# Seven products instead of eight blocks for a third pair of w_down blocks, and the query tiles in a shared pool

## The chip, the cores and the metric

The kernel runs on one core of one Trainium2 chip, in one launch. The metric is the device time in microseconds (us). The engines named here are TensorE (PE in the rows, its weight loads PEld), VectorE (DVE), ScalarE (ACT), GpSimd (POOL), and SyncE (SP), which issues most of the DMAs.

## What is computed

Two layers of a trunk with three token mixers, an MLP and an embedding gate, all in fp32. The change lies in the MLP; its other half moves two tiles of the attention branch. The reference, cut to these:

```python
for i in range(DEPTH):                       # DEPTH = 2, h is (1, 256, 1024)
    u = rms_norm(h, norm_mix_g[i])
    proj = u @ w_in[i]
    ...                                      # pooling, gated convolution, differential attention (q, k, v)
    h = h + merged @ w_o[i]
    m = rms_norm(h, norm_mlp_g[i])
    h = h + jnp.square(jax.nn.relu(m @ w_up[i])) @ w_down[i]      # 1024 -> 4096 -> 1024
    e = rms_norm(h, norm_ple_g[i])
    h = h + jax.nn.sigmoid(e @ w_ple_gate[i]) * (p[i] @ w_ple_proj[i])
```

## The kernel before

Every product of fp32 numbers is made from three: an operand is split into a rounded high part and the remainder, and high by high, high by low and low by high are summed in PSUM. Activations are split once. Weights are streamed from HBM and split on the way: `WeightStream` loads them in transfers of two units of 128x1024 numbers into three staging buffers; for each unit ACT copies the high part (`whi`, L285) and DVE subtracts it (`wlo`, L286). The two parts go to one of six buffers (`AHEAD + 1`, L197, L207), so a unit is split up to five units ahead of its matmuls, and its buffer is free once the unit six places before it has been read. `weight_plan` lists the units in the order in which PE takes them; transfers are issued in that order.

The MLP of a layer has eight blocks b of 512 hidden columns. Block 0 comes first, in four units of their own shape. For each other block there are four "up" units, `("up", b, m)`, of 128 hidden columns: 16 matmuls (`unit_c`, L487) into one PSUM bank of the pool `bp`, which has four banks. `relu_sq_c` (L1128) follows an up unit: ACT copies the bank, and after the second of two units DVE adds, ACT does a relu and two squares, and DVE subtracts; this leaves the block's squared activations as a high part and a remainder (`st["s", b]`), and, for a block whose pair is in `GROUPS`, the squares themselves (`st["f", b]`).

The way back down has two forms. Directly, `("down", b, f)` is two units of kind A, each 12 matmuls of 512 columns (`unit_a`, L436), for one half f of the output columns; a block has two of these. A pair of blocks j, j+1 whose j is in `GROUPS` is done by Strassen's seven products `("S", j, n)` instead of eight block products: each product is two units of kind S, each six matmuls of 512 columns (`unit_s`, L459). Around the products stand

- four operands of the activations (`operands`, L1169, steps 0 to 3, for products 5, 6, 3 and 7 in that order): a sum or difference on DVE, a copy of its high part on ACT (L537), the remainder on DVE (L538). They are attached to the four units that follow the last up unit of block j+1;
- the weights. Products 2 and 3 use plain blocks through the staging buffers. The others use two 1 MB tiles, `self.sums`: two blocks are loaded into them (L233), DVE adds them after product 1 was split (L265), and POOL issues DMAs that add further blocks to them (`add_to`, L256), one after the split of each of the products 1, 5 and 6. The tiles are free for the next pair (`sums_busy`) once product 4 has been split; until then `load` (L219) stops at the next pair's product 1;
- what happens to the results (`product_out`, L1212): products 1, 6 and 7 run up one sum in one bank ("chain"), from which DVE takes parts after each; product 5 is copied by ACT; 2, 3 and 4 go into the accumulators of the direct units.

Before the change the pairs (0,1) and (4,5) are done so, the blocks 2, 3, 6 and 7 directly, and `mlp_order` (L59) writes the order of ups, products and downs out by hand. Side work is attached to a unit and comes in program order behind it; the Tile framework then orders the instructions of each engine by a priority that follows the program, and gives out buffers from pools. `u4` (8 buffers) holds tiles of 128x1088 numbers: the split and squared activations, the copies of the up units, and in the mixers the operands of the branches. The split queries `qT` are two constant tiles of their own, written in `qk_transpose` (L659) and read in `probs` (L736).

## Time and profile before

| what | value |
|---|---|
| time, median of 3 runs | 841.7 us (841.66 to 843.43) |
| time of the profiled execution | 842.62 us |
| its span | 840.7 us |
| PE busy | 832.3 us, 99% |
| DVE busy | 669.1 us, 80% |
| ACT busy | 563.9 us, 67% |
| TensorE clock granted | 1.00 in all forty slices |
| moved by DMA | 177.29 MB, 211 GB/s |

The span is the time from the first to the last instruction that the profiler saw; the profiled execution's own time is 1.9 us longer. The share of an engine is its busy time over the span. Matmuls are pipelined, so that the times of single matmuls overlap: what one costs is read from the distance of two starts.

### The profile page before, as it was taken

The numbers are of one execution on the slowest core, as the hardware profiler recorded it, in microseconds if no ns is written. First come the engines' busy times: TensorE is split into PE (matmuls) and PEld (weight loads), VectorE is DVE, ScalarE is ACT, GpSimd is POOL, SyncE is SP. The second block draws the span as 40 slices with busy tenths as digits, with TensorE's granted clock in tenths as the row PEclk, the third lists the DMA queues.
The fourth block names the chain that finished last, engine by engine and source line by source line (L and its number), as shares of the span: only waits on it lengthen the run. The fifth ranks groups of instructions, "written<-read, shape, count | busy, mean of one in ns | idle before, by whom it ended". The sixth has DMA issues, their size and how long they took to land.

```text
span 840.7 us, 11223 instructions
## 1 busy us (share of the span) xinstructions
PE 832.3 (99%) x4236; PEld 706.5 (84%) x4236; DVE 669.1 (80%) x926; ACT 563.9 (67%) x821; POOL 46.2 (5%) x52
## 2 busy tenths in 40 slices
PE   8999999999999999999999999999999999999997
PEld 7888888788988888888878888888889888888886
DVE  5989989876679667977678798998766886688864
ACT  6867566654678667976666756666546876688662
POOL 2400000000000000000023000000000000000000
PEclk9999999999999999999999999999999999999999
DMA  9864539764758766966546455586655778668531
GB/s 330 308 232 150 226 107 293 209 217 177 272 161 262 243 241 186 266 195 209 184 165 223 172 170 232 137 244 220 216 184 226 249 208 256 244 200 245 191 133 51
DMA packets 27126, 177.29 MB, mean 211 GB/s; under 512 B 3136, under 2 KB 4032, under 8 KB 6464
## 3 DMA queue, kind: packets, MB, share of 16 engines
q1 hardware_dynamic: 24192, 157.53, 51.3%
q0 software_dynamic: 2592, 18.88, 12.0%
q8 instruction: 33, 0.54, 0.2%
q10 hardware_dynamic: 288, 0.18, 0.1%
q14 instruction: 21, 0.17, 0.1%
HBM read 175.52 MB, written 1.05 MB: 210 GB/s over the span
## 4 chain that ended last, share of the span: by engine, by line
PE 97%; DMA 1%; ACT 1%; DVE 0%; issue 0%; ACTq 0%
PE acc L445 38%; PE bp L493 19%; PE bp L495 10%; PE bp L445 6%; PE acc L464 3%; PE acc L466 3%; PE acc L468 3%; PE acc L456 2%; PE bp L468 2%; PE bp L466 2%; PE bp L464 2%; PE tr L516 1%; PE acc L1309 1%; PE bp L482 1%; PE bp L484 1%; PE bp L480 1%
## 5 line engine op out<-in xcount | busy, mean ns | idle before, releaser
L286 DVE TENSOR_TENSOR wlo<-stage,whi 128x1024 fp32r<-128x1024 f32 (+1 forms) x272 | 328.3, 1213 | 111.2 <-ACT whi L285 109.7
L285 ACT CAST whi<-stage 128x1024 fp32r<-128x1024 f32 (+1 forms) x272 | 282.8, 1045 | 188.6 <-PE acc L445 81.7
L445 PE MATMUL acc<-whi,t 128*128 128x512 f32 x928 | 299.0, 392 | 0.0
L445 PEld LDWEIGHTS acc<-whi,t 128*128 128x128 f32 x928 | 173.6, 188 | 34.9 <-ACT whi L285 0.2
L493 PE MATMUL bp<-t,whi 128*128 128x512 f32 x704 | 192.3, 394 | 0.0
L445 PE MATMUL acc<-wlo,t 128*128 128x512 f32 x464 | 181.4, 391 | 0.0
L493 PEld LDWEIGHTS bp<-t,whi 128*128 128x128 f32 x704 | 122.2, 189 | 18.0
L495 PEld LDWEIGHTS bp<-t,wlo 128*128 128x128 f32 x704 | 107.9, 189 | 14.7
L495 PE MATMUL bp<-t,wlo 128*128 128x256 f32 x704 | 112.4, 281 | 0.0
L445 PEld LDWEIGHTS acc<-wlo,t 128*128 128x128 f32 x464 | 87.2, 188 | 17.3 <-DVE wlo L286 0.2
L286 DVE TENSOR_TENSOR wlo<-t,whi 128x1024 fp32r<-128x1024 f32 x60 | 73.0, 1221 | 14.7 <-ACT whi L285 13.7
L285 ACT CAST whi<-t 128x1024 fp32r<-128x1024 f32 x60 | 63.0, 1052 | 29.6 <-PE acc L445 9.3
L256 POOL DMA_DIRECT2D t<-in_w_dram x18 | 15.9, 884 | 474.5 <-DVE wlo L286 159.1
L464 PE MATMUL acc<-whi,t 128*128 128x512 f32 x104 | 40.6, 391 | 0.3 <-ACT t L989 0.3
L445 PE MATMUL bp<-whi,t 128*128 128x512 f32 x128 | 40.7, 389 | 0.0
L466 PE MATMUL acc<-wlo,t 128*128 128x512 f32 x104 | 40.6, 390 | 0.0
L468 PE MATMUL acc<-whi,t 128*128 128x512 f32 x104 | 40.5, 390 | 0.0
L506 ACT ACTIVATE t<-tr,par 128x256 fp32r<-128x256 f32 (+1 forms) x56 | 26.2, 501 | 15.0 <-PE tr L516 11.0
L507 DVE SCALAR_TENSOR_TENSOR t<-tr,par,t 128x256 fp32r<-128x256 f32 (+1 forms) x56 | 27.9, 525 | 6.8 <-ACT t L506 6.5
L1135 ACT COPY t<-bp 128x512 f32<-128x512 f32 x56 | 32.1, 577 | 0.0
L445 PEld LDWEIGHTS bp<-whi,t 128*128 128x128 f32 x128 | 24.0, 188 | 5.1 <-ACT t L537 0.2
L468 PE MATMUL bp<-whi,t 128*128 128x512 f32 x64 | 25.1, 393 | 0.0
(178 smaller groups left out, 1004.3 us busy)
## 6 DMA issues: line engine op xcount, KB each, us to landing
stage<-in_w_dram SPq DMA_DIRECT2D x131, 1024.0 KB, 4.8
t<-in_w_dram POOLq DMA_DIRECT2D x18, 1024.0 KB, 8.5
t<-in_w_dram SPq DMA_DIRECT2D x12, 1024.0 KB, 6.0
stage<-in_w_dram SPq DMA_DIRECT2D x6, 512.0 KB, 5.8
stage<-in_w_dram SPq DMA_DIRECT2D x4, 256.0 KB, 4.3
h<-in_x_dram SPq DMA_DIRECT2D x4, 256.0 KB, 10.2
t<-in_xT_dram SPq DMA_DIRECT2D x1, 512.0 KB, 8.6
out_dram<-h SPq DMA_DIRECT2D x2, 256.0 KB, 2.0
```

Source lines behind the costliest of these rows:

```text
L285: self.nc.scalar.copy(out=hi[:, cs], in_=src[:, cs])
L286: self.nc.vector.tensor_sub(out=lo[:, cs], in0=src[:, cs], in1=hi[:, cs].bitcast(F32))
L445: nc.tensor.matmul(accs[t], lhsT=lhs[:, kx + j, tk], rhs=rhs[:, j, :], start=begins[t] and j == 0 and n == 0, stop=last and j == 1 and n == 2,
L456: nc.tensor.matmul(accs[half][t], lhsT=lhs[:, k, t * P:(t + 1) * P], rhs=rhs[:, 0, cs], start=k == 0 and n == 0, stop=False)
L464: nc.tensor.matmul(bank, lhsT=xh[:, k + n, :], rhs=wh[:, n, :], start=first, stop=False, skip_group_check=True)
L466: nc.tensor.matmul(bank, lhsT=xh[:, k + n, :], rhs=wl[:, n, :], start=False, stop=False, skip_group_check=True)
L468: nc.tensor.matmul(bank, lhsT=xl[:, k + n, :], rhs=wh[:, n, :], start=False, stop=k + n == 3, skip_group_check=True)
L493: nc.tensor.matmul(bank, lhsT=wh[:, k, :], rhs=xk[k], start=k == 0, stop=False, skip_group_check=True)
L495: nc.tensor.matmul(bank[:, 1, :], lhsT=wl[:, k, :], rhs=xk[k][:, 0, :], start=False, stop=k == KD - 1, skip_group_check=True)
L506: nc.scalar.activation(out=hi, in_=src, func=AF.Copy, scale=g)
L507: nc.vector.scalar_tensor_tensor(out=lo, in0=src, scalar=g, in1=hi.bitcast(F32), op0=ALU.mult, op1=ALU.subtract)
L1135: nc.scalar.copy(out=both[:, :, m % 2, :], in_=tiles.pop(("bp", "up", j, m)))
```

## The change

- `GROUPS` gains the pair (2,3). Per layer eight A units of w_down (blocks 2 and 3, both halves, two units each) go, and seven products of two S units each come, with their operands, weight sums and results. The blocks 6 and 7 stay direct.
- `mlp_order` is written anew: `up(b, *ms)` names single up units, and the 21 products stand between them, mostly behind one or two up units each.
- `qT` is allocated from `u4` in each layer, when the first queries are written, and `u4` has ten buffers instead of eight.

```diff
--- before.py
+++ after.py
@@ -32,7 +32,7 @@
 UNIT_COLS = {"A": 512, "B": 256, "C": 128, "D": 1024, "P": 512, "S": 512}
 
 
-GROUPS = (0, 4)
+GROUPS = (0, 2, 4)
 
 GATED = 0
 
@@ -58,8 +58,8 @@
 
 def mlp_order():
 
-    def up(b, half):
-        return [("up", b, m) for m in (2 * half, 2 * half + 1)]
+    def up(b, *ms):
+        return [("up", b, m) for m in ms]
 
     def down(b, f):
         return [("down", b, f)]
@@ -67,13 +67,14 @@
     def prod(j, *ns):
         return [("S", j, n) for n in ns]
 
-    order = up(0, 0) + up(0, 1) + up(1, 0) + up(1, 1)
-    order += up(2, 0) + prod(0, 1) + up(2, 1) + up(3, 0) + prod(0, 5) + down(2, 0) + up(3, 1) + prod(0, 3)
-    order += down(2, 1) + prod(0, 6) + down(3, 0) + up(4, 0) + prod(0, 7) + down(3, 1) + prod(0, 2)
-    order += up(4, 1) + up(5, 0) + prod(0, 4) + up(5, 1)
-    order += up(6, 0) + prod(4, 1) + up(6, 1) + prod(4, 5) + up(7, 0) + prod(4, 3) + up(7, 1) + prod(4, 6)
-    order += down(6, 0) + prod(4, 7, 2) + down(6, 1) + prod(4, 4) + down(7, 0) + down(7, 1)
-    return order
+    order = up(0, 0, 1, 2, 3) + up(1, 0, 1) + prod(0, 1) + up(1, 2, 3) + up(2, 0, 1) + prod(0, 5) + up(2, 2) + prod(0, 3)
+    order += up(2, 3) + up(3, 0) + prod(0, 6) + up(3, 1) + prod(0, 7) + up(3, 2) + prod(0, 2) + up(3, 3) + prod(0, 4)
+    order += up(4, 0, 1) + prod(2, 1) + up(4, 2, 3) + prod(2, 5) + up(5, 0) + prod(2, 3) + up(5, 1, 2) + prod(2, 6)
+    order += up(5, 3) + prod(2, 7) + up(6, 0) + prod(2, 2) + up(6, 1, 2) + prod(2, 4)
+    order += up(6, 3) + prod(4, 1) + up(7, 0, 1) + prod(4, 5) + up(7, 2) + prod(4, 3) + up(7, 3) + down(6, 0)
+    order += prod(4, 6) + down(6, 1) + prod(4, 7, 2)
+    return order + prod(4, 4) + down(7, 0) + down(7, 1)
+
 
 
 A_IN, C_X, C_B, C_C, Q, K, V, GATE = (MIX * i for i in range(8))
@@ -339,7 +340,7 @@
     const = ctx.enter_context(tc.tile_pool(name="const", bufs=1))
     ws = WeightStream(ctx, tc, w)
     u8 = ctx.enter_context(tc.tile_pool(name="u8", bufs=4))
-    u4 = ctx.enter_context(tc.tile_pool(name="u4", bufs=8))
+    u4 = ctx.enter_context(tc.tile_pool(name="u4", bufs=10))
     u2 = ctx.enter_context(tc.tile_pool(name="u2", bufs=17))
     sm = ctx.enter_context(tc.tile_pool(name="sm", bufs=4))
     ps_acc = ctx.enter_context(tc.tile_pool(name="ps_acc", bufs=4, space=bass.MemoryType.PSUM))
@@ -412,7 +413,6 @@
     invcnt = csb[:, CC_INV:CC_INV + 4 * PAD].rearrange("p (g t) -> p g t", t=PAD)
     mhalf = const.tile([P, 16], F32, tag="mhalf", name="mhalf")
     nc.gpsimd.memset(mhalf, -0.5)
-    qT = [const.tile([P, NH, S], F32R, tag=f"qT{j}", name=f"qT{j}") for j in range(2)]
 
 
     lam = const.tile([P, DEPTH], F32, tag="lam", name="lam")
@@ -660,6 +660,9 @@
             tk = slice(t * P, (t + 1) * P)
             tr = head_transpose(qkr.pop((nm, t)))
             if nm == "q":
+                if t == 0:
+                    st["qT"] = [t4v(F32R) for _ in range(2)]
+                qT = st["qT"]
                 gain_split(qT[0][:, :, tk], qT[1][:, :, tk], tr, par[:, i, PC_QG:PC_QG + 1])
                 return
             for a in range(2):
@@ -738,7 +741,7 @@
             nk = (t + 1) * P
             scv = acc_tile().rearrange("p (h a k) -> p h a k", h=nh, a=2)
             for n, hd in enumerate(heads):
-                qh, ql = [q[:, hd, t * P:(t + 1) * P] for q in qT]
+                qh, ql = [q[:, hd, t * P:(t + 1) * P] for q in st["qT"]]
                 kh, kl = [k[:, hd, :, 0:nk] for k in st["kp"]]
                 nc.tensor.matmul(scv[:, n], lhsT=qh, rhs=kh, start=True, stop=False)
                 nc.tensor.matmul(scv[:, n], lhsT=qh, rhs=kl, start=False, stop=False)
```

## Rows read from the trace of the kernel before

**Rows 1.** the page: busy time of each engine, and the chain's shares by engine

```profile
PE 832.3 (99%) x4236; PEld 706.5 (84%) x4236; DVE 669.1 (80%) x926; ACT 563.9 (67%) x821; POOL 46.2 (5%) x52
...
PE 97%; DMA 1%; ACT 1%; DVE 0%; issue 0%; ACTq 0%
```

**Rows 2.** waits of PE, whole span: engine, line, awaited; us, times, longest

```profile
PE acc L456 <- ACT t L506: 1.7, 2, 1.2
...
PE acc L464 <- ACT t L989: 0.3, 1, 0.3
```

**Rows 3.** chain of work in order of time: start us, us, what

```profile
281.06 5.44 PE acc L445 x24
```

**Rows 4.** timeline of PE around one product: start us, us, engine line

```profile
308.30 0.39 PE L464 MATMUL acc<-whi,t 128*128 128x512 f32 x1
...
311.01 1.07 PE L493 MATMUL bp<-t,whi 128*128 128x512 f32 x4
```

**Rows 5.** timeline of all engines, from up(1,3)'s end to pair 0's first operand

```profile
244.74 1.09 PE L493 MATMUL bp<-t,whi 128*128 128x512 f32 x4
...
246.87 0.68 DVE L1141 TENSOR_TENSOR t<-t 128x512 f32<-128x512 f32 x1
...
247.55 1.09 PE L493 MATMUL bp<-t,whi 128*128 128x512 f32 x4
...
250.35 0.40 PE L464 MATMUL bp<-whi,t 128*128 128x512 f32 x1
...
250.56 0.70 DVE L1146 TENSOR_TENSOR t<-t,t 128x512 fp32r<-128x512 f32 x1 [0.97 <-ACT t L1145]
...
251.17 0.69 DVE L1175 TENSOR_TENSOR t<-t,t 128x512 f32<-128x512 f32 x1
...
252.91 0.61 ACT L537 CAST t<-t 128x512 fp32r<-128x512 f32 x1
...
253.12 1.07 PE L493 MATMUL bp<-t,whi 128*128 128x512 f32 x4
...
254.17 1.21 DVE L286 TENSOR_TENSOR wlo<-t,whi 128x1024 fp32r<-128x1024 f32 x1
...
255.30 0.68 DVE L538 TENSOR_TENSOR t<-t,t 128x512 fp32r<-128x512 f32 x1
```

**Rows 6.** DVE by form, MLP of layer 0 (222 to 386 us)

```profile
L286 DVE TENSOR_TENSOR wlo<-stage,whi 128x1024 fp32r<-128x1024 f32 x53 | 64.4, 1222 | 21.0 <-ACT whi L285 20.6
...
L265 DVE TENSOR_TENSOR t<-t,t 128x2048 f32<-128x2048 f32 x2 | 4.6, 2289 | 0.0
...
L1209 DVE SCALAR_TENSOR_TENSOR h<-bp,r,h 128x512 f32<-128x512 f32 x4 | 3.0, 743 | 0.0
```

**Rows 7.** busy time by stretch: PE, PEld, DVE, ACT, POOL, clock, DMA

```profile
222.00:386.00 164.00, 164.00 (x872) 141.15 (x871) 130.10 (x143) 121.20 (x166) 5.25 (x6) 1.00 0.71 224
...
340.00:360.00 20.00, 20.00 (x110) 17.20 (x109) 19.00 (x24) 18.51 (x28) 0.88 (x1) 1.00 0.91 242
```

**Rows 8.** timeline of PE in the first up units: order of issue

```profile
230.05 0.28 PE L480 MATMUL bp<-t,whi 128*128 128x256 f32 x1
230.17 1.09 PE L493 MATMUL bp<-t,whi 128*128 128x512 f32 x4
231.10 0.28 PE L482 MATMUL bp<-t,whi 128*128 128x256 f32 x1
```

**Rows 9.** the page: DMA queues; the commonest load, its median us to landing

```profile
q1 hardware_dynamic: 24192, 157.53, 51.3%
q0 software_dynamic: 2592, 18.88, 12.0%
...
stage<-in_w_dram SPq DMA_DIRECT2D x131, 1024.0 KB, 4.8
```

**Rows 10.** timeline of SP's queue: the two loads of pair 4's sums

```profile
291.97 0.33 SPq L233 DMA_DIRECT2D t<-in_w_dram  x1
...
313.56 0.33 SPq L233 DMA_DIRECT2D t<-in_w_dram  x1
```

## The prediction, made before the changed kernel was run

> **What bounds the kernel now.** I read the busy times first, then the waits of PE, then the chain, and only then single stretches. PE is busy for 99% of the span and makes 97% of the chain that ended last [rows 1]. Busy time alone would prove little, because the times of pipelined matmuls overlap; so the second view matters more: in the whole span PE waited five times, 3.8 us in all (the largest 1.7, the smallest 0.3), each time in a stage that the change does not touch [rows 2]. In both MLPs it never waits. There the spacing of matmuls is the time: 24 matmuls of 512 columns take 5.44 us, 0.227 us each [rows 3]. DVE is the next engine: 130 of 164 us in the MLP of layer 0, 79%, and 19 of 20 us in its fullest stretch, where PE still does not wait [rows 7]. So matmuls that vanish shorten the kernel one for one, as long as DVE, ACT and the DMAs still keep ahead. The whole question is whether they do.
>
> **What PE loses.** Eight A units go per layer. An A unit is 12 matmuls, half of the 5.44 us of 24: 2.72 us [rows 3]; eight are 21.8. Seven products come, 12 matmuls each. A product behind a direct unit takes 2.71 us [rows 4], one behind an up unit 2.77 (250.35 to 253.12) [rows 5]. In the new order nearly every product stands behind an up unit, so 7 x 2.77 = 19.4. The difference is 2.4 us per layer, 4.8 for two. The bounds: 2.7 per layer if the switch between shapes costs nothing more, 2.1 if all 21 products pay 0.06 more than they did and nothing is given back. I take 4.8.
>
> By the Trainium skill's page "TensorE: Matmul & The Clock Gate" (Back-to-back issue gap) a sustained stream of 512-column matmuls is spaced about 131 ns; 24 fewer would then give an estimate of 3.1 us instead of 5.4. The row disagrees: 227 ns here, with PE waiting for nothing.
>
> **What DVE gains in work, per layer.** From starts that follow one another without idling: a weight remainder 1.13 us (254.17 to 255.30), a 512-column operation 0.61 (250.56 to 251.17) [rows 5]; the big weight sum 2.29 and a residual update 0.74 by their durations [rows 6]. Six more units to split (14 for 8): 6.8. Four operands, two operations each: 4.9. Results of products 1, 6 and 7: four residual updates and two additions, 4.2. One weight sum: 2.3. Together 18.2, on 130: 148 of some 162 us, 91%.
>
> The mean hides where it falls. Take the stretch from the end of pair 0's product 1 to the end of pair 2's product 4, 47 units. PE needs 21 up units x 2.81 (244.74 to 247.55 [rows 5]) + 13 products x 2.77 = 95.0. DVE needs 47 remainders (53.1), ten relu pairs (12.2), twelve operands, since pair 4's fall in here too (14.6), seven residual updates and four additions of results (7.6), two weight sums (4.6): 92.1, or 97%. Against this stands the lead: a unit is split five units ahead. Five units of this stretch (two ups, three halves of products) last 9.7 us, less 2.3 for the copy and the remainder: about 7 us by which DVE may be late. Adding the same durations unit by unit in the new order, and taking off what PE needs for each, its backlog comes to at most 5 us, around pair 2's products 7 and 2. So I cost the work on DVE at nothing; its cover is that lead. ACT gets six copies of some 1 us and five shorter ones, 9 on 121 [rows 7]: 80%, likewise nothing.
>
> **What the DMAs gain.** On SP nothing in bytes: eight half-megabyte units go, two loads of sums and two staged megabytes come. On POOL three adding DMAs per layer, 3.1 MB. POOL's queue took 12.0% of 840.7 us for 18.9 MB [rows 9], 5.3 us per MB, so 17 us per layer; the share of the engines in the MLP rises from 0.71 to about 0.82. A stretch at 0.91 made no wait [rows 7]. Nothing.
>
> **What is moved closer.** Four distances shrink.
> 1. *Pair 0's first operand.* Before, from the end of up(1,3) at 244.74 to the end of the remainder at 255.98 it took 11.2 us: relu chain to 251.17, then sum, copy and remainder, 2.8 us of it queued behind other work on ACT and DVE [rows 5]. Product 5 came far later, so nobody waited. Now only up(2,0) and up(2,1) stand between: 5.6 us, plus 0.5 until the remainder is read, 6.1. The chain is short by 2.3 (nothing queued) to 5.2 us (as before). But PE's order is not the program's: four matmuls of up(1,0) were issued in the midst of block 0's last units [rows 8], because the framework fills a gap that it foresees with later work that is ready. up(2,2), 2.81 us, is ready behind product 5. With it the loss is 0 to 2.4 us per layer, to 5.2 without.
> 2. *Product 7 behind product 6* waits until DVE has taken the sum from the bank; one up unit, 2.81 us, stands between in pairs 0 and 2. A remainder that is under way and the addition are 1.13 + 0.61 = 1.7. Nothing, with 1.1 to spare; a loss as large as DVE's further lateness without it.
> 3. *The weight sums are reloaded* for pair 4 with one up unit between pair 2's product 4 and its product 1. Split of product 4, a load of 4.8 us [rows 9], the next split of 2.3: 7.1, against 7.4 + 1.4 + 2.8 = 11.6 with full lead. It spares 4.5, about DVE's backlog there; a loss of 0 to 2 us per layer. The second sum is free earlier and was loaded 21.6 us before the first [rows 10], so one megabyte counts, not two.
> 4. *Pool of ten.* At up(4,1) the split activations of blocks 2, 3 and 4, three tiles of squares and one copy are alive: ten, just enough. In the mixers ten less two queries are the eight of before. Nothing; the cover is that PE has no wait there.
>
> For 1 to 3 together I take 0.5 us per layer, near the lower ends, since PE's order bends and DVE was caught up in most places. Sum: 840.7 - 4.8 + 1.0 = 836.9 of span; with the 1.9 us around it 838.8 against 842.6 of this execution. That execution is 0.9 above the median, so 837.9 against 841.7.
>
> **The rivals.**
> - *The operand is late* (point 1). For it: 11.2 us against 6.1 and nothing in the edit that speeds the chain. Against it: rows 8, and two more buffers, so copies of up units may come sooner. With up(2,2) taken ahead at most 2.4 us per layer are lost, about what is won: 840 to 842.5. Without it 10.4 - 4.8: 847.
> - *DVE becomes the bound, and it is slower.* Place: the 47 units. DVE seldom runs without holes, since remainders wait for ACT's copies (21 us idle before 53 of them [rows 6]). If it can be filled only to 85%, between the 79% of the MLP and the 95% of the fullest 20 us, it needs 108.4 us; less 95.0 and the lead of 7, that is 6.4 lost per layer: 841.7 - 4.8 + 12.8 = 849.7. It decides at 88%: below that the loss exceeds 2.4. Against it: 95% for 20 us without a wait. The Trainium skill's "Perfetto Trace Analysis" (Identifying the Most-Contended Engine) judges TensorE by its weight loads, not by matmul time; by this PE has 16% of headroom (84% in rows 1), and DVE, at 91% of the MLP, would be the engine to relieve, not to load. The missing waits of PE speak against it.
> - *The reload of sums* (point 3), up to 2 us per layer: 838 to 841.
> - *It does not do what it says:* a pool that is one short or a wait in the mixers eats the gain: 841 to 843.
>
> **How the numbers follow.** Forecast, stalls of up to 1.7 us per layer: 836.3 to 839.9, chance 0.64. Late operand in part, reload or pool: 840 to 843, 0.21. Late operand in full 0.05, DVE as the bound 0.10: 845 to 850. About 0.2% (1.7 us) is what a measurement of this kernel can tell from no change. So faster 0.65, same 0.21, slower 0.14. The range leaves out the last two cases and goes down to 835.8, all of 2.7 per layer and no stall with some spread.
>
> **What would show it.** PE should have 24 matmuls fewer and 5 us less busy time; each MLP should be 1.5 to 2.4 us shorter. PE's waits should name little in the MLP: L538 or L537 before pair 0's product 5 is rival one; `wlo` spread over the blocks 3 to 6 is rival two; `whi` before pair 4's product 1, with a load behind it, is the reload. DVE should be at 90% or more of the MLP. I am wrong in the mechanism if the matmuls go and PE's waits in the MLP grow to more than 2.4 us per layer.

## The result, and the profile after

The changed kernel takes 854.68 us (median, 853.80 to 855.66) against 842.57 us (841.66 to 843.51) for the kernel before, taken beside it: a ratio of 1.0145, interval 1.0133 to 1.0158. It is slower by 12.1 us where a gain of 3.8 was forecast. The profiled execution took 854.15 us with a span of 852.3, 11.6 more than before. In the rows of the changed kernel a line of before has a number that is 1 higher up to L414, the same from there to L660, and 3 higher behind it.

The page, the rows that answer to [rows 1] and [rows 9]: busy time, DMA queues, and the commonest loads (their last number is the median time to landing).

```profile
PE 832.6 (98%) x4212; PEld 705.9 (83%) x4212; DVE 701.0 (82%) x968; ACT 574.9 (67%) x843; POOL 54.8 (6%) x58
...
q1 hardware_dynamic: 25632, 157.53, 49.9%
q0 software_dynamic: 3456, 25.17, 15.6%
...
stage<-in_w_dram SPq DMA_DIRECT2D x117, 1024.0 KB, 4.9
t<-in_w_dram POOLq DMA_DIRECT2D x24, 1024.0 KB, 8.8
```

The 24 matmuls are gone (4212 for 4236), the six adding DMAs have come. By the page alone little else is new: every engine's share moved by 2 points at most, and the medians to landing lie within 0.3 us of those of before (4.8 and 8.5). The waits of PE tell more (engine, line, awaited: us in total, times, longest), beside [rows 2]:

```profile
PE bp L464 <- ACT whi L286: 4.2, 1, 4.2
PE bp L464 <- ACT t L537: 3.8, 2, 1.9
PE bp L493 <- ACT t L1138: 2.6, 1, 2.6
PE acc L464 <- ACT t L992: 1.8, 2, 1.3
PE acc L464 <- ACT whi L286: 1.4, 1, 1.4
PE tr L394 <- POOL mhalf L415: 1.0, 1, 1.0
PE acc L456 <- ACT t L506: 0.5, 1, 0.5
```

They add up to 15.3 us against 3.8. The first three rows are in the MLP, where PE had not waited: before pair 0's product 5 in both layers (1.89 us each), and in pair 2 (2.63 us at 308 in layer 0, 4.17 us at 734 in layer 1). The next two rows are three waits at the gates of the mixers (1.26 us in layer 0, 1.45 and 0.50 in layer 1). Then the stretches around the two waits in pair 2, in the columns of [rows 7] (the number after POOL's count is the granted clock, then the DMA share), with the whole MLP of layer 0 first:

```profile
222.00:386.00 164.00, 159.48 (x842) 136.91 (x841) 141.12 (x160) 125.05 (x175) 7.86 (x9) 0.99 0.76 231
300.00:320.00 20.00, 17.37 (x85) 14.56 (x84) 16.58 (x22) 13.46 (x21) 1.54 (x2) 0.91 0.93 252
720.00:740.00 20.00, 15.83 (x72) 13.17 (x71) 15.94 (x19) 11.81 (x18) 1.73 (x2) 0.83 0.90 247
```

In them the clock was granted at 0.91 and 0.83, where all slices of before had 1.00. That is the lower of the two levels, 1.2 GHz, for some microseconds; it began shortly behind the end of the wait in layer 0 and shortly before it in layer 1. The loss is 20 x 0.09 and 20 x 0.17 us, 5.1 together before rounding. In layer 1 the lower level began 1.2 us before the wait ended, and half of that is no loss of its own, so that some 4.5 us come on top of the waits (1.7 and 2.8). On PE's timeline of layer 0 one sees both, the wait and then a group of four matmuls that takes 1.91 us where the same group took 1.09 in [rows 5]:

```profile
308.01 1.19 PE L493 MATMUL bp<-t,whi 128*128 128x512 f32 x4 [2.63 <-ACT t L1138]
309.04 0.75 PE L495 MATMUL bp<-t,wlo 128*128 128x256 f32 x4
309.59 1.91 PE L493 MATMUL bp<-t,whi 128*128 128x512 f32 x4
```

So the 11.6 us of span come out: 11.5 more of waits, 4.5 of half clock, and by subtraction 4.4 less for the rest, which is near the 4.8 forecast for the matmuls.

Why PE waited at 308.01 stands on ACT's timeline:

```profile
301.87 0.62 ACT L1148 ACTIVATE t<-t 128x512 f32<-128x512 f32 x1
306.43 1.04 ACT L286 CAST whi<-stage 128x1024 fp32r<-128x1024 f32 x1 [3.95 <-DMA stage<-in_w_dram]
307.38 0.58 ACT L1138 COPY t<-bp 128x512 f32<-128x512 f32 x1
...
312.47 2.00 ACT L286 CAST whi<-t 128x1024 fp32r<-128x1024 f32 x2 [2.56 <-DMA t<-in_w_dram]
```

ACT kept to its order. From 302.5 it stood still before the copy of a weight unit that PE would need only at 312.15, because its load had not landed; the copy that empties a PSUM bank (L1138) stood behind it, and PE had no free bank. Of ACT's waits in the MLP of layer 0, 18.1 us are for DMAs:

```profile
ACT whi L286 <- DMA stage<-in_w_dram: 10.6, 5, 3.9
ACT whi L286 <- DMA t<-in_w_dram: 7.5, 4, 3.0
```

In the MLP of layer 0 before there was no such wait, in layer 1 one of 2.8 us, at which PE did not wait. And 7.0 of the 18.1 us come after 340 us, in pair 4, where PE does not wait either; so such a wait cost time here only where what stood behind it in ACT's order was what PE needed next. In layer 1 PE's wait is of the other kind: ACT waited 3.34 us until 732.75 for the addition that makes product 6's sum (issued at 720.26, landed after 12.42 us), and PE for ACT. The load that was late in layer 0 was issued at 296.05, between pair 2's first two adding DMAs, here POOL's timeline from 290 to 325:

```profile
295.42 0.87 POOL L257 DMA_DIRECT2D t<-in_w_dram  x1 [29.26 <-DVE t L266]
299.79 0.88 POOL L257 DMA_DIRECT2D t<-in_w_dram  x1 [3.50 <-DVE wlo L287]
316.21 0.87 POOL L257 DMA_DIRECT2D t<-in_w_dram  x1 [15.54 <-DVE wlo L287]
```

In the kernel before, POOL's timeline from 320 to 350 shows the first two additions of pair 4:

```profile
330.36 0.88 POOL L256 DMA_DIRECT2D t<-in_w_dram  x1 [49.01 <-DVE t L265]
339.11 0.88 POOL L256 DMA_DIRECT2D t<-in_w_dram  x1 [7.88 <-DVE wlo L286]
```

There they are 8.75 us apart, and the first landed after 8.62 us, before the second was issued. Now the two are 4.4 us apart, so the second is issued while the first is under way. By the trace they landed after 10.73 and 12.61 us, and the load between them after 10.30, where the median of such a load is 4.9. The view of the DMAs from 290 to 306 us, cut to it, shows the same: a line of 40 slices of 0.4 us with the busy share in tenths, and the issues in that stretch.

```profile
DMA  0000000010000000099359919879593996949299
...
t<-in_w_dram POOLq DMA_DIRECT2D x2, 1024.0 KB, 11.7
stage<-in_w_dram SPq DMA_DIRECT2D x1, 1024.0 KB, 10.3
```

For the first 6.8 us almost nothing moves, since the staging buffers were full: from 280 to 310 us SP's queue waited for DVE to be done with one, once for 9.8 us.

```profile
SPq L251 <- DVE wlo L287: 22.7, 4, 9.8
```

Then two additions and the loads come at once. A share averaged over 20 us shows neither the hole nor the heap.

The changed kernel's own pair 4 shows that the heap alone is not enough. POOL's timeline there:

```profile
347.36 0.88 POOL L257 DMA_DIRECT2D t<-in_w_dram  x1 [30.28 <-DVE t L266]
353.60 0.87 POOL L257 DMA_DIRECT2D t<-in_w_dram  x1 [5.36 <-DVE wlo L287]
```

The stretch behind it, in the columns of [rows 7]:

```profile
360.00:380.00 20.00, 20.00 (x93) 16.62 (x92) 15.64 (x18) 15.12 (x21) 0.87 (x1) 1.00 1.01 317
```

These additions overlap too (6.2 us apart, 8.72 and 10.74 us to landing), the loads issued beside them took 8.02 to 10.06 us, the DMA share is 1.01, and PE did not wait. In pair 2 the slow load was the first one behind the hole, and its copy stood in front of the one that frees a bank.

### The profile page after: what moved, and what is told of

Its sections match the earlier page's. It is cut to its first block, busy times and chain, and to the rows that moved or that the text cites. A ratio compares the mean times of both kernels' runs of the same rounds, so it can differ in the third digit from the quotient of the medians.

```text
span 852.3 us, 11278 instructions
## 1 busy us (share of the span) xinstructions
PE 832.6 (98%) x4212; PEld 705.9 (83%) x4212; DVE 701.0 (82%) x968; ACT 574.9 (67%) x843; POOL 54.8 (6%) x58
## 3 DMA queue, kind: packets, MB, share of 16 engines
q0 software_dynamic: 3456, 25.17, 15.6%
## 5 line engine op out<-in xcount | busy, mean ns | idle before, releaser
L287 DVE TENSOR_TENSOR wlo<-stage,whi 128x1024 fp32r<-128x1024 f32 (+1 forms) x264 | 316.9, 1211 | 79.6 <-ACT whi L286 78.7
L445 PE MATMUL acc<-whi,t 128*128 128x512 f32 x800 | 257.0, 393 | 0.0
L445 PEld LDWEIGHTS acc<-whi,t 128*128 128x128 f32 x800 | 149.7, 188 | 29.9
L445 PE MATMUL acc<-wlo,t 128*128 128x512 f32 x400 | 156.5, 392 | 0.0
L287 DVE TENSOR_TENSOR wlo<-t,whi 128x1024 fp32r<-128x1024 f32 x80 | 96.0, 1220 | 25.8 <-ACT whi L286 25.4
L286 ACT CAST whi<-t 128x1024 fp32r<-128x1024 f32 x80 | 82.1, 1049 | 47.6 <-DMA t<-in_w_dram 22.8
L445 PEld LDWEIGHTS acc<-wlo,t 128*128 128x128 f32 x400 | 75.2, 188 | 14.6 <-DVE wlo L287 0.2
L464 PE MATMUL acc<-whi,t 128*128 128x512 f32 x128 | 50.2, 392 | 3.2 <-ACT t L992 1.8
L468 PE MATMUL acc<-whi,t 128*128 128x512 f32 x128 | 50.0, 390 | 0.0
L466 PE MATMUL acc<-wlo,t 128*128 128x512 f32 x128 | 50.0, 390 | 0.0
L464 PE MATMUL bp<-whi,t 128*128 128x512 f32 x96 | 38.2, 398 | 8.0 <-ACT whi L286 4.2
L1138 ACT COPY t<-bp 128x512 f32<-128x512 f32 x56 | 32.4, 578 | 13.0 <-PE bp L495 13.0
L445 PE MATMUL bp<-whi,t 128*128 128x512 f32 x128 | 41.1, 389 | 0.0
L506 ACT ACTIVATE t<-tr,par 128x256 fp32r<-128x256 f32 (+2 forms) x60 | 29.2, 516 | 13.5 <-PE tr L516 7.1
L466 PE MATMUL bp<-wlo,t 128*128 128x512 f32 x96 | 37.6, 392 | 0.0
L468 PE MATMUL bp<-whi,t 128*128 128x512 f32 x96 | 37.6, 392 | 0.0
```

The lines of the kernel that those rows point to most:

```text
L286: self.nc.scalar.copy(out=hi[:, cs], in_=src[:, cs])
L287: self.nc.vector.tensor_sub(out=lo[:, cs], in0=src[:, cs], in1=hi[:, cs].bitcast(F32))
L445: nc.tensor.matmul(accs[t], lhsT=lhs[:, kx + j, tk], rhs=rhs[:, j, :], start=begins[t] and j == 0 and n == 0, stop=last and j == 1 and n == 2,
L464: nc.tensor.matmul(bank, lhsT=xh[:, k + n, :], rhs=wh[:, n, :], start=first, stop=False, skip_group_check=True)
L466: nc.tensor.matmul(bank, lhsT=xh[:, k + n, :], rhs=wl[:, n, :], start=False, stop=False, skip_group_check=True)
L468: nc.tensor.matmul(bank, lhsT=xl[:, k + n, :], rhs=wh[:, n, :], start=False, stop=k + n == 3, skip_group_check=True)
```

## The experiments

All were timed beside the kernel before (842.05 to 842.51 us in the several comparisons). "Waits" is the sum of PE's waits in the profiled execution (before 3.8, changed kernel 15.3), "clock" half of the time for which the lower clock was granted while PE was not waiting (0 and 4.5), so that nothing is counted twice.

| run | edit | us | ratio (interval) | waits | clock |
|---|---|---|---|---|---|
| e1 | kernel before, only the query tiles and ten buffers | 847.51 | 1.006 (1.0041 to 1.008) | 6.0 | 0 |
| e2 | pair 2's first addition left out | 845.56 | 1.0035 (1.0022 to 1.0048) | 9.3 | 0 |
| e3 | pair 0's product 5 one up unit later | 853.3 | 1.0137 (1.0119 to 1.0155) | 14.7 | 4.5 |
| e4 | wider distances all over the order | 871.64 | 1.0364 (1.0336 to 1.0393) | 31.3 | 3.9 |
| e5 | query tiles constant, nine buffers | 860.22 | 1.0211 (1.0186 to 1.0237) | 16.9 | 5.8 |
| e6 | pair 2's first addition later in the program | 856.53 | 1.0164 (1.0145 to 1.0182) | 15.7 | 8.0 |
| e7 | e3, e5 and e6 together | 858.39 | 1.0187 (1.0166 to 1.0207) | 16.9 | 7.2 |
| e8 | e7, pair 2's product 1 one unit earlier | 875.52 | 1.0385 (1.0358 to 1.0412) | 33.4 | 8.1 |
| e9 | query tiles constant, eight buffers | 872.35 | 1.036 (1.0343 to 1.0376) | 27.2 | 12.4 |
| e10 | less work on DVE | 859.11 | 1.0208 (1.0189 to 1.0226) | 17.8 | 5.0 |
| e11 | pair 2's first addition held back | 849.52 | 1.0087 (1.0072 to 1.0102) | 11.8 | 1.7 |
| e12 | e3, e9 and e11 together | 856.37 | 1.0176 (1.0155 to 1.0198) | 17.7 | 4.6 |
| e13 | ten buffers as a pool of eight and one of two | 857.41 | 1.0179 (1.0157 to 1.02) | 20.5 | 1.9 |
| e14 | e3, e11 and e13 together | 850.89 | 1.0104 (1.0087 to 1.0121) | 9.3 | 4.5 |
| e15 | e11 and e13 together | 852.4 | 1.0115 (1.0097 to 1.0132) | 10.9 | 3.3 |
| e16 | e3 and e11 together | 850.59 | 1.0095 (1.0067 to 1.0122) | 10.5 | 4.4 |
| e17 | e2 and e3 together | 848.32 | 1.0059 (1.0035 to 1.0082) | 9.3 | 1.6 |
| e18 | e16, pair 2's product 6 one up unit later | 860.23 | 1.0207 (1.019 to 1.0224) | 18.8 | 7.7 |

From this profile my theory had three causes: pair 2's two additions that meet the loads, the pool of ten that reorders the mixers, and pair 0's late operand. The main rival was DVE, now at 86% of the MLP.

### Pair 2's additions: e2, e10, e6, e11

**e2** leaves one of the two additions out.

```diff
         if prod == 1:
             self.nc.vector.tensor_add(out=fst, in0=fst, in1=snd)
-            self.add_to(snd, i, j, 1, 1)
+            if j != 2:
+                self.add_to(snd, i, j, 1, 1)
```

> The changed kernel without pair 2's first adding DMA (the one behind product 1), so product 7 of the blocks 2 and 3 works on a wrong sum of weights. Theory: the two adding DMAs of pair 2, issued 4 to 5 us apart beside staging loads, slow each other to 10 to 12.6 us, and what waits for them (the copies of the next weights on ACT, then PE) makes PE's waits of 2.6 us (layer 0) and 4.2 us (layer 1) and, behind them, 10 us at half clock. Without one of them the waits and the half clock go: 854.7 - 6.8 - 5.1 = 843, 841 to 845. Rival: DVE is the bound there, and a DMA less changes nothing: 852 or more, with waits of like size in the blocks 4 and 5.

It took 845.56 us, 9.1 less than the changed kernel. The same two stretches, by busy time:

```profile
300.00:320.00 20.00, 20.00 (x106) 17.01 (x105) 20.00 (x25) 17.59 (x27) 1.75 (x2) 1.00 0.86 227
720.00:740.00 20.00, 19.61 (x102) 16.41 (x101) 19.57 (x23) 16.93 (x26) 0.86 (x1) 1.00 0.93 275
```

PE is busy throughout or nearly so, the clock is full, and DVE at 20.00 of 20 us holds nobody up. One addition of 1 MB per layer carried waits of 6.4 us and all of the half clock. The first load behind the hole, which took 10.30 us in the changed kernel, is issued at 296.89 here and lands after 4.59, and the addition that is left lands after 8.36, although DVE is busy throughout.

**e10** takes work from DVE instead.

```diff
-            parts = [t2(F32R).rearrange("p (k t) -> p k t", t=P) for _ in range(2)]
-            split(*parts, d)
+            if j:
+                hi = t2(F32R).rearrange("p (k t) -> p k t", t=P)
+                nc.scalar.copy(out=hi, in_=d)
+                parts = [hi, hi]
+            else:
+                parts = [t2(F32R).rearrange("p (k t) -> p k t", t=P) for _ in range(2)]
+                split(*parts, d)
```

> The changed kernel; left out are the remainders of the operands of the pairs 2 and 4 (the high part is used twice, so the products are less exact): 8 operations of 0.61 us on DVE per layer, 4.9 us less on DVE in the MLP, no DMA and no matmul less. Theory (the crowded adding DMAs make the waits in pair 2): the two waits of 2.63 and 4.17 us and the half clock behind them stay, each within 1 us; 852 to 855 us. Rival (DVE is late): they go by more than half; 846 to 850 us.

The waits of PE, in its three longest groups:

```profile
PE bp L493 <- ACT t L1138: 6.5, 2, 3.5
PE bp L464 <- ACT t L537: 3.8, 2, 1.9
PE acc L464 <- ACT t L992: 1.8, 2, 1.3
```

The waits in pair 2 stay (2.96 and 3.54 us for 2.63 and 4.17) though DVE works 8.6 us less in the two layers (692.4 us busy for 701.0): DVE is not what PE waits for there. The time, 859.11, is 4.4 above the changed kernel, and outside of what either theory gave; the other waits are longer too (17.8 us in all), and why is open.

**e6** moves the call of that addition behind the one that follows product 5.

> The changed kernel with one DMA of pair 2 issued later and nothing left out: the adding DMA for product 7 goes behind the one for product 6, that is behind the split of product 5 instead of product 1. Theory: it was in the way of the one that product 6 waits for; that one lands in 8.5 to 9.5 us instead of 12.5, product 7 has time, the waits of 2.6 and 4.2 us and the half clock go as in the run without it: 843, 842 to 847. Rival: the bytes themselves are too many for that stretch, whatever their order; then product 7 or a staged block waits instead: 850 or more.

```diff
         elif prod == 5:
             self.add_to(fst, i, j, 1, 1)
+            if j == 2:
+                self.add_to(snd, i, j, 1, 1)
```

It says nothing: the framework's order is not the program's, the addition that was ready went first again, and the two were issued at 296.95 and 301.32 and landed after 10.71 and 12.57 us, as before the edit. **e11** makes the order a dependency: a DVE operation on one column of the destination reads product 5's split (and adds 0 times it), and the addition comes after.

```diff
         elif prod == 5:
             self.add_to(fst, i, j, 1, 1)
+            if j == 2:
+                self.nc.vector.scalar_tensor_tensor(out=snd[:, 0:1], in0=self.parts[u][1][:, 0:1].bitcast(F32),
+                                                    scalar=0.0, in1=snd[:, 0:1], op0=ALU.mult, op1=ALU.add)
+                self.add_to(snd, i, j, 1, 1)
```

> The changed kernel, but pair 2's first adding DMA goes behind the second one and behind product 5's split, held there by a small DVE operation on its destination. Theory (the coincidence of the two additions with the stage loads makes the wait): the stage loads in that stretch land in under 9 us, the waits of 2.63 and 4.17 us go below 1 us, no half clock there; 845.5 to 848 us. Rival (the sum of DMA work in the stretch counts, not the coincidence): the waits move to product 7 or 6 and stay, 853 to 856 us.

POOL's timeline from 290 to 325 us:

```profile
299.13 0.87 POOL L257 DMA_DIRECT2D t<-in_w_dram  x1 [33.15 <-DVE wlo L292]
302.81 0.87 POOL L257 DMA_DIRECT2D t<-in_w_dram  x1 [2.80 <-DVE t L272]
312.02 0.87 POOL L257 DMA_DIRECT2D t<-in_w_dram  x1 [8.35 <-DVE wlo L292]
```

849.52 us, 5.2 less than the changed kernel with all of the work done. The two waits in pair 2 are gone (0.36 us is left), and two of 1.28 and 0.75 us come in pair 4. But the reason that I gave is only half right: the additions still overlap (8.17, 12.65 and 12.80 us to landing in layer 0) and the loads beside the last two take 10.86 to 12.32 us, not under 9. The heap stays and has moved by some 4 us, and the first load behind the hole, issued at 295.39, now has nearly nothing beside it and lands after 4.66 us. That is what e2 and e11 have in common. What a slow load costs depends on which unit it brings and on when ACT gets to it.

### The pool: e1, e5, e9, e13

**e1** is the kernel before with the second half of the change alone.

```diff
-    u4 = ctx.enter_context(tc.tile_pool(name="u4", bufs=8))
+    u4 = ctx.enter_context(tc.tile_pool(name="u4", bufs=10))
...
-    qT = [const.tile([P, NH, S], F32R, tag=f"qT{j}", name=f"qT{j}") for j in range(2)]
...
+                if t == 0:
+                    st["qT"] = [t4v(F32R) for _ in range(2)]
+                qT = st["qT"]
```

> The kernel before with the other half of the change alone: the query tiles from the pool of ten, no third pair, the old order. Theory: the move is neutral, since the pool minus the two query tiles is the old eight; within 1 us of the kernel before (842 to 844) and the waits of PE around the gate products stay at 0.3 us. Rival: the move reorders the mixers and makes the 2.9 us of waits on product operands that the changed kernel shows around its gate products; then 844 to 847.

847.51 us, 5.5 more than before; I had expected nothing. PE's longest waits are those at the gates, in both layers, that the changed kernel has too:

```profile
PE acc L463 <- ACT t L991: 1.8, 2, 1.3
PE acc L463 <- ACT whi L285: 1.4, 1, 1.4
```

DVE's timeline says why. First the kernel before, then e1 (L921 and L923 are the first step of the convolution, L957 and L959 the first of the running sums that the gates need):

```profile
122.92 0.68 DVE L957 TENSOR_TENSOR t<-t,t 128x512 f32<-128x512 f32 x1
...
132.80 1.13 DVE L921 TENSOR_SCALAR t<-t,par 128x256 f32<-128x256 f32 x4
```

```profile
115.61 1.14 DVE L923 TENSOR_SCALAR t<-t,par 128x256 f32<-128x256 f32 x4
...
125.74 0.69 DVE L959 TENSOR_TENSOR t<-t,t 128x512 f32<-128x512 f32 x1
```

With eight buffers the sums go first; with ten the convolution starts 17 us sooner, ahead of the sums, which come 2.8 us later, and PE waits at the gates. That the convolution lacked a buffer before is my reading: DVE does not wait at it in the trace, since the framework has laid the order down beforehand. That the number of buffers decides it is shown by e5 and e9. The profiled execution of e1 was the fastest of its four (845.75; the others up to 848.89), with 2.2 us more of waits and a span longer by 3.0; what the slower ones add, no trace shows. Of the 12.1 us by which the changed kernel is slower, 6.6 are left for the third pair if e1's 5.5 are taken off.

**e5** keeps the query tiles as constants and gives the pool nine.

```diff
-    u4 = ctx.enter_context(tc.tile_pool(name="u4", bufs=10))
+    u4 = ctx.enter_context(tc.tile_pool(name="u4", bufs=9))
...
+    qT = [const.tile([P, NH, S], F32R, tag=f"qT{j}", name=f"qT{j}") for j in range(2)]
```

> The changed kernel with the query tiles constant as before and nine buffers in the pool (ten do not fit beside them): the third pair without the move. Theory: the move alone cost 5.5 us, so without it the waits on product operands around the gates (1.3 us in layer 0, 1.9 in layer 1) go, the MLP stays: 854.7 - 5.5 = 849, 848 to 852. Rival: a ninth buffer is enough to give the mixers the other order of instructions; the gate waits stay and the time with them: 853 or more.

860.22 us, and the waits at the gates stay (1.46, 1.48 and 1.45 us): one buffer more is enough, the queries are not the cause. **e9** goes down to eight, by the same edit with `bufs=8`.

> The changed kernel with the query tiles constant again and the pool of eight buffers that the kernel before has. Theory (what reorders the mixers is the number of buffers; eight give back the order of before): the waits of PE at the gates (1.26 us in layer 0, 1.45 and 0.50 in layer 1) go, about 849 to 851 us. In the MLP ten tiles of this size are alive at the block 4, so eight may cost it 0 to 3 us of new waits there. Rival (the third pair itself moves the mixers): the waits at the gates stay, 854 to 860 us.

The waits at the gates go (0.27 us is left), as the theory had it. The MLP pays for it, not with the 0 to 3 us that I allowed: its waits are 25.1 us where the changed kernel has 10.6, the longest 7.66, and half clock takes another 12.4. Eight are too few for it. **e13** gives the mixers eight and the MLP ten.

```diff
-    u4 = ctx.enter_context(tc.tile_pool(name="u4", bufs=10))
+    u4 = ctx.enter_context(tc.tile_pool(name="u4", bufs=8))
+    q4 = ctx.enter_context(tc.tile_pool(name="q4", bufs=2))
...
-                    st["qT"] = [t4v(F32R) for _ in range(2)]
+                    st["qT"] = [q4v(F32R) for _ in range(2)]
...
-                st["s", j] = (t4v(F32R), t4v(F32R))
+                t = q4v if j in (0, 4) else t4v
+                st["s", j] = (t(F32R), t(F32R))
```

> The changed kernel, its ten buffers split into a pool of eight, as the mixers had before, and a pool of two, which the query tiles use in the mixers and the split activations of blocks 0 and 4 in the MLP. Theory (more than eight shared buffers reorder the mixers; ten are needed in the MLP): no wait at the gates over 0.4 us, the waits in the MLP as in the changed kernel (1.89, 2.63, 1.89, 4.17), 849 to 851 us. Rival (the order of the mixers changes with any change of the MLP): the waits at the gates stay, 853 to 857 us.

Again no wait at the gates over 0.3 us, so what reorders the mixers is the number of buffers that their tiles share. But the time is 857.41 us, and the longest group of PE's waits is now this one, which holds 6.64 and 1.59 us before pair 2's product 5:

```profile
PE bp L468 <- ACT t L541: 12.0, 4, 6.6
```

Before the wait of 6.64 us ACT makes the copy of product 5's operand at 308.06, where it was at 298.25 in the changed kernel, and it stood still for 3.93 us for a staged load just before. That two buffers which only some tiles may use are worth less than two shared ones fits this, but no trace separates it from the late load. That the 5.5 us of e1 would come back as a whole when the mixers are mended was therefore not shown by any run.

### The late operand, and where its gain goes: e3, e16, e17, e18

**e3** puts one more up unit ahead of pair 0's product 5.

```diff
-... + up(2, 0, 1) + prod(0, 5) + up(2, 2) + prod(0, 3)
+... + up(2, 0, 1, 2) + prod(0, 5) + prod(0, 3)
```

> The changed kernel with pair 0's product 5 one up unit later, behind up(2,2). Theory: its two waits on the operand's copy (1.9 us in each layer) go, as the copy came 7.6 us after up(1,3) and 8.4 us now stand between: 854.7 - 3.8 = 851, 850 to 852.5. Rival: the operand chain is stretched by the load on ACT and DVE and the wait moves to product 3, now directly behind: 853.5 or more.

Both waits of 1.89 us are gone, and the time is 853.3, only 1.4 lower: the wait in pair 2 of layer 0 grew from 2.63 to 4.51 us. **e16** does the same with the addition held back, **e17** with it left out, to see whether the heap of additions takes the gain.

> The changed kernel (pool of ten) with pair 2's first addition held back as in e11 and pair 0's product 5 behind one more up unit as in e3. Theory (the operand is a cause of its own; in e3 the crowd took the gain back): 849.5 - 3.8 = 845.7 us, 844 to 847. Rival (the gain is given back here too): 848 to 852 us, with a wait of 2 to 5 us in pair 2.

> The changed kernel with pair 2's first addition left out, as in e2 (product 7 of the blocks 2 and 3 uses a wrong weight sum), and pair 0's product 5 behind one more up unit. Theory (the operand, the additions and the pool are three separate causes): 845.6 - 3.8 = 841.8 us, 840.5 to 843, with only the waits at the gates left. Rival: 844 to 847 us, new waits in pair 2 without any crowd of additions.

The heap alone is not what takes it. e16 took 850.59 us (e11 849.52), with new waits of 2.93 and 2.48 us in pair 2; e17 took 848.32 us (e2 845.56), with 2.02 and 2.21. In the latter the first addition is not there, and still this is ACT's timeline:

```profile
302.27 1.06 ACT L287 CAST whi<-stage 128x1024 fp32r<-128x1024 f32 x1
307.67 2.00 ACT L287 CAST whi<-t 128x1024 fp32r<-128x1024 f32 x2 [4.34 <-DMA t<-in_w_dram]
```

The copy at 307.67 is that of product 6, out of the sum to which an addition was issued at 298.41, right after product 5's remainder; it landed at 307.59 after an ordinary 9.18 us. So there is a chain, split of product 5, addition into the same tile, split of product 6, and if PE comes to pair 2 earlier by 1.9 us it waits there instead. The executions of e17 lie apart (843.97 and 844.33, the others 847.09 to 849.76); the profiled one is of the lower, so its rows explain only a part of the median.

**e18** gives this chain one more up unit, on top of e16.

```diff
-... + up(5, 1, 2) + prod(2, 6)
-order += up(5, 3) + prod(2, 7) + up(6, 0) + prod(2, 2) + up(6, 1, 2) + prod(2, 4)
+... + up(5, 1, 2, 3) + prod(2, 6)
+order += up(6, 0) + prod(2, 7) + up(6, 1) + prod(2, 2) + up(6, 2) + prod(2, 4)
```

> As e16, with pair 2's product 6 one up unit later (behind up(5,3)), and product 7 and 2 one up unit later with it. Theory (the chain through the first sum, from product 5's split over an addition of 9.5 us to product 6's split, is too long for the units between; one up unit is 2.8 us, its waits of 2.93 and 2.48 us go, and with them the half clock behind them): 850.6 - 5.4 - 5.1 = 840 us, 839 to 844. Rival (the next stage load or sum is late instead): 847 to 853 us, with waits of 2 us or more in pair 2 or 4.

The rival won, 860.23 us. ACT's timeline in pair 2:

```profile
303.08 1.06 ACT L291 CAST whi<-stage 128x1024 fp32r<-128x1024 f32 x1
311.59 1.04 ACT L291 CAST whi<-stage 128x1024 fp32r<-128x1024 f32 x1 [7.45 <-DMA stage<-in_w_dram]
312.54 1.04 ACT L291 CAST whi<-t 128x1024 fp32r<-128x1024 f32 x1
```

Now the sum is in time and the staged unit that took its place in the order is late: its load was issued at 300.61 and took 10.90 us between two additions (9.16 and 12.61). PE waited 4.23 us, until the copy of product 6's sum behind it was made. One thing clouds the rest of this run: pair 4's operands are made in the four units behind up(5,3), so that here the last of them takes the place of pair 2's, and the second half of pair 2's product 7 is computed with it; the wait shown comes before that.

### All at once: e4, e7, e8, e12, e14, e15

Six orders and mixtures tried to mend several causes together; none is faster than the kernel before, or than e11.

**e4** changed the order so:

```diff
-... + up(2, 0, 1) + prod(0, 5) + up(2, 2) + prod(0, 3)
-order += up(2, 3) + up(3, 0) + prod(0, 6) + up(3, 1) + prod(0, 7) + up(3, 2) + prod(0, 2) + up(3, 3) + prod(0, 4)
-order += up(4, 0, 1) + prod(2, 1) + up(4, 2, 3) + prod(2, 5) + up(5, 0) + prod(2, 3) + up(5, 1, 2) + prod(2, 6)
-order += up(5, 3) + prod(2, 7) + up(6, 0) + prod(2, 2) + up(6, 1, 2) + prod(2, 4)
+... + up(2, 0, 1, 2) + prod(0, 5) + up(2, 3) + prod(0, 3)
+order += up(3, 0, 1) + prod(0, 6) + up(3, 2) + prod(0, 7, 2) + up(3, 3) + prod(0, 4)
+order += up(4, 0) + prod(2, 1) + up(4, 1, 2, 3) + prod(2, 5) + up(5, 0) + prod(2, 3) + up(5, 1, 2, 3) + prod(2, 6)
+order += up(6, 0) + prod(2, 7, 2) + up(6, 1, 2) + prod(2, 4)
```

> The changed kernel with the same units in another order: pair 0's product 5 one up unit later, in pair 2 three ups instead of two between products 1 and 5 and three instead of two between 5 and 6, so that its adding DMAs lie 8 us apart. Theory (late operand, crowded adds): both kinds of wait in the MLP go, 854.7 - 3.8 - 11.9 = 839, with what is left of waits in the mixers 838 to 842. Rival (DVE at its limit over the 47 units): the waits come back in other places, 848 or more.

It took 871.64 us with waits of 11.08 and 11.68 us, and has the flaw told of e18, so it says little on distances. **e7** is e3 with the edits of e5 and e6; **e8** puts pair 2's product 1 one unit earlier as well:

```diff
-order += up(4, 0, 1) + prod(2, 1) + up(4, 2, 3) + prod(2, 5) + ...
+order += up(4, 0) + prod(2, 1) + up(4, 1, 2, 3) + prod(2, 5) + ...
```

> The changed kernel with three mendings: query tiles constant and nine buffers, pair 0's product 5 one up unit later, pair 2's first adding DMA behind product 5. Theory (operand, crowded adds and the move explain all of it): what is left is the shorter matmul work, 842.1 - 4.8 = 837, with small waits 836 to 840. Rival (DVE or the bytes are the bound and the waits wander): 843 or more.

> As the kernel with three mendings, and pair 2's product 1 one up unit earlier, so that its sums are reloaded with one up unit between but product 5 has three ups behind product 1. Theory: if adds still meet in the other they are further apart here: 836 to 839, up to 1.5 us under the other. Rival: the reload has too little time and product 1 waits up to 2 us per layer: 838 to 842, over the other.

They took 858.39 and 875.52 us; since e6's edit did nothing, neither has the heap removed. In e8, with the additions 6.2 us apart (295.85 and 302.02, landing after 10.83 and 12.30 us), a load beside them took 15.32 us, ACT stood still for 7.62 and 4.25 us and PE for 11.75. More distance between the two products that call for the additions did not help. **e12** (e3, e9, e11), **e15** (e11, e13) and **e14** (e3, e11, e13) have the addition really held back:

> The changed kernel with the three causes taken away: pool of eight with constant query tiles, pair 2's first addition held back as in e11, pair 0's product 5 behind one more up unit as in e3. Theory (the causes add up): 854.7 - 5.5 - 9.1 - 3.8 = 836.3 us, with 0 to 3 us of waits for buffers in the MLP 836 to 840, faster than the kernel before. Rival (each saving is given back in the next crowded stretch, as in e3 and e7): 843 to 850 us.

> The changed kernel with the two pools of e13 and pair 2's first addition held back as in e11. Theory: 849.5 - 5.5 = 844 us (842.5 to 845.5), with the waits of 1.89 us before pair 0's product 5 the largest that are left. Rival: as e11, 848 to 851 us.

> As e15, and pair 0's product 5 behind one more up unit. Theory (the causes add up): e15 less 3.8 us and less the half clock, about 838 to 842 us, no slower than the kernel before. Rival (the time is given back in the crowded stretch of pair 2, as in e3): 843 to 848 us.

856.37, 852.4 and 850.89 us. In each the causes that the edit aims at are gone (no wait at the gates over 0.3 us in any of them; no wait before pair 0's product 5 in e12 and e14), and in each pair 2 has a new wait for an operand's copy, 2.6 us in layer 0 of all three; whether the other buffers or the earlier start bring it is not separated. The theory that the causes add up is refuted by these three, and by e16 and e17.

## Why the prediction was wrong, step by step

- **What bounds the kernel; what PE loses.** Right in kind, and a little high in size. 24 matmuls are gone. The spans, less their waits and their half clock, lie below that of before by 4.4 us in the changed kernel and by 1.7 to 5.3 in e2 to e18, 3.4 in the mean, where 4.8 was forecast; e1, with the matmuls of before, lies 0.9 above, which shows how rough this is. The lower bound of 2.1 per layer does not follow from its own words: if the 14 products that were there paid 0.06 more each, 2.4 would go down to 1.5.
- **What DVE gains.** Right in its result, and a little high in size: 31.9 us for the two layers where 36.4 were forecast, and 86% of the MLP (141.1 us of the stretch of 164 in [rows 7], where 130 were) and not 90% or more. It did not become the bound: e10 took work from it and the waits stayed; in e2 it is busy for 20.00 of 20 us without harm. By the rule in the Trainium skill's "Perfetto Trace Analysis" (Identifying the Most-Contended Engine), which the prediction weighed, TensorE with its weight loads at 83% of that stretch would have room and DVE, at 86%, would be the one to relieve; relieving it brought nothing here.
- **What the DMAs gain.** This is the step that failed first. The engine time was right (25.17 MB in 15.6% of the span is again 5.3 us per MB), and the share of the MLP was even below the forecast (0.76 against 0.82). But "a stretch at 0.91 made no wait" proved nothing. What counted is when a load lands, not how busy the engines are: before, the first two additions of pair 4 came 8.75 us apart, the second after the first had landed, at 8.62 and 8.88 us to landing, and the loads beside them took 7.3 to 8.4; in pair 2 they come 4.4 apart, out of 6.8 us in which almost nothing moved, and land after 10.73 and 12.61, the load between them after 10.30. "Nothing" was 6.8 us of waits in pair 2 and 4.5 of half clock. I priced the added bytes and never the instants at which POOL would issue them.
- **The path from a late load to PE** was missing. I took the lead of five units, 7 us, as cover for DVE, put ACT at nothing by its busy share, and never asked what stands behind a late load in ACT's order. The copy for a unit stands in ACT's order five units ahead, in front of the copies that empty PSUM; when its load is late, ACT stops long before PE needs the unit, and PE stops for a bank. e2 and e11 show it by its absence: there the load is in time and the wait is gone.
- **What is moved closer, 1.** The range was right: the high part of the operand was ready 7.6 us after the end of up(1,3), PE did take up(2,2) ahead, behind product 5's first two matmuls, and the loss of 1.89 us per layer lies in the 0 to 2.4 given. The term in the sum was too small: 0.5 us per layer for the points 1 to 3 together. And my later inference that removing the wait would give it back was wrong (e3, e16, e17).
- **2 and 3.** Nothing was seen of 2. Product 7 did not wait for product 6, and PE has no wait in the changed kernel's pair 4. The chain that does bind in pair 2 when PE is early was not on the list: product 5, addition, product 6, with three up units and a product between, against four up units and a product in pair 4 of before. It lies in what the reordering moved closer. Pair 0 has three up units and a product there too, without a wait, so the distance alone does not decide.
- **4, the pool of ten.** Failed: "nothing" was 5.5 us (e1). The argument that PE has no wait there shows that there was no queue for a buffer that hurt; it does not show that the want of a buffer had no use. In e1's rows its going brings the convolution ahead of the gates' operands. And "ten, just enough" was so tight that eight, or eight and two, came out slower than ten with the waits at the gates (e9, e13).
- **The clock.** Not in the sum at all: 4.5 of the 11.6 us. PE never fell to the lower level in the kernel before, so no row gave its price; that a wait can bring it, and that the two stalls of 6.8 us then cost 11.3, had to be a bound.
- **The rivals.** None was what happened as a whole. "The operand is late" came true with its sign (L537 before product 5), for 3.8 of the 11.5 us of waits. "It does not do what it says" named the pool, at 841 to 843 us, where e1 has 847.5; the forecast for slower rested on DVE. The prediction's own sign of a wrong mechanism came out: PE's waits in the MLP are 4.5 us in layer 0 and 6.1 in layer 1, over the 2.4 given.

What stays open: whether any order keeps the gain of the third pair. The best that was run with all of the work done is e11, 849.52 us, still 0.9% slower than before; e2 and e17 lie lower, but leave an addition out. In pair 2 three suppliers (staged loads, the sums, the operands) are each just in time, and each edit that relieved one made the next late; no run shows one of them alone as the limit. How much of e1's 5.5 us is the wait at the gates is open too, since its trace accounts for 2.2.

## What to carry to other kernels

Price an added DMA by when it is issued and by what lands beside it: look in the trace for the instants at which its queue can issue, and for the load whose copy stands first in an in-order engine's way. A full pool may be what keeps two chains in their good order; more buffers are a change of order, to be costed like one. When several suppliers are just in time, a wait removed upstream is no gain until the next one's slack is known.

## What the runs showed of the hardware

- At PE's waits of 2.63 and 4.17 us the granted clock was at the lower level for some microseconds (0.91 and 0.83 over 20 us), which cost 1.7 and 2.8 us on top; in e9, with two waits of 1.89 us and four of 3.25 to 7.66, 12.4 us were lost so in all. The length of a wait does not decide: the waits of 1.89 us in the changed kernel and in e2 were followed by full clock, those in e9 by the lower level; in e12 waits of 2.61 and 2.64 us were followed by full clock, in e14 one of 2.62 by the lower level.
- An addition of 1 MB landed 8.6 us after its issue in the kernel before; of two issued 4.4 us apart the first took 10.7 and the second 12.6 us, and a plain load of 1 MB issued between them 10.3 instead of the median of 4.9; in e8 one took 15.32.
- The share of the DMA engines in the stretches with the longest waits, 0.93 and 0.90, was about the 0.91 of the fullest stretch of the MLP before, which had none; in pair 4 of the changed kernel it was 1.01 over 20 us, and PE did not wait.
